# A softmax over 32768 columns: transfers of whole half rows in three buffers, in an order written out

## The chip, the core and the metric

The kernel runs on one core of one Trainium2 chip. The metric is the device time of one execution in microseconds (us). Three executions of the kernel before took 2491.85, 2492.3 and 2493.0 us; the median is 2492.3 us.

## The reference, cut to what matters

```python
logits = np.random.randn(16, 256, 32768).astype(np.float32); temperature = 1.0
scaled = logits / temperature
scaled = scaled - scaled.max(axis=-1, keepdims=True)
exp_scaled = np.exp(scaled)
return (exp_scaled / exp_scaled.sum(axis=-1, keepdims=True)).astype(np.float32)
```

There are 4096 rows of 32768 float32 values. Each row is read once and written once: 536.87 MB in, 536.87 MB out.

## The kernel before, in words

A row of 32768 values is cut into two half rows of 16384 values (64 KB), and each half row lies in one of the 128 partitions of the on-chip memory. So 64 rows make a **group** of 128 half rows, 8.4 MB, and there are 64 groups (`G`). The two halves of a row lie in neighbouring partitions.

A group is loaded, worked on in place and stored as two **chunks** (`C` = 2) of 8192 columns: 128 partitions of 32 KB each, 4.2 MB. The on-chip tensor `X` holds six chunks (`_BUFS`), which is three groups. Chunk i lies in buffer i modulo 6.

All transfers, loads (`load`, L113) and stores (`store`, L128), are issued by SyncE, in one queue and in program order. The page calls SyncE's queue SPq. A load first waits until the store that used its buffer last has landed, and a store waits until VectorE has scaled its chunk. At the start six loads are issued. After that, the main loop issues for each chunk i its store and then the load of chunk i + 4 (`_LEAD`). The first and the last group are loaded, and the last one stored, in pieces of 4096 columns (`_EDGE`).

For each group (`compute`):
- VectorE takes the negated maximum of a chunk (L156), and ScalarE then replaces the chunk by the exponentials of its values less that maximum, and adds them up (L170). Each chunk has a maximum and a sum of its own.
- When ScalarE is done with the last chunk, VectorE exchanges the small results between the two partitions of a row (L183, a shuffle) and finds the maximum of the row (L187); ScalarE computes a correction factor for each chunk (L194); VectorE adds the corrected sums (L200) and takes the reciprocal (L212).
- VectorE multiplies each chunk by its factor and by the reciprocal (L221). This is what a store waits for.

VectorE works through one group after the other and waits in place for ScalarE before the shuffle. In the last group the three steps on columns go in four pieces of 4096 columns instead of two of 8192.

A transfer of 128 partitions is spread over the core's 16 DMA engines. Each of them moves eight rows, a row of the transfer being one packet, and then adds one to the transfer's semaphore, a packet of a few bytes which is called a count here. A transfer has landed when all 16 counts have arrived. Each engine goes through its own list and does not wait for the others.

Of the kernel before, what the change touches and what calls it, by code (L numbers as in the profile page):

```python
# [6 lines left out]


_CW = 8192
_BUFS = 6  # L10
_LEAD = 4
_EDGE = 4096


class Stream:
# [7 lines left out]

    def wait(self, *tokens):
        need = {}
        for t in tokens:
            for sem, value in t if isinstance(t, list) else [t]:
                key = id(sem)
                if value > max(self.seen.get(key, 0), need.get(key, (None, 0))[1]):
                    need[key] = (sem, value)  # L30
        for key, (sem, value) in need.items():
            self.engine.wait_ge(sem, value)  # L32
            self.seen[key] = value
# [4 lines left out]
        return (self.sem, self.count)  # L38


class Landing:


    def __init__(self, nc, name):
        self.sem = nc.alloc_semaphore(name)
        self.count = 0

    def add(self, instruction):
        self.count += 16
        instruction.then_inc(self.sem, 16)  # L50

    def token(self):
        return (self.sem, self.count)


@with_exitstack
def kernel(
# [6 lines left out]
    nc = tc.nc  # L64
    inv_t = 1.0 / float(temperature)
    P = nc.NUM_PARTITIONS
    fp32 = mybir.dt.float32
    Exp = mybir.ActivationFunctionType.Exp
    A = mybir.AluOpType
# [1 line left out]
    xf = logits.flatten_outer_dims()  # L71
    of = out.flatten_outer_dims()
    N, V = xf.shape
    W = V // 2
    C = W // _CW
    assert W * 2 == V and C * _CW == W and (N * 2) % P == 0
    x = xf.rearrange("n (h v) -> (n h) v", h=2)
    o = of.rearrange("n (h v) -> (n h) v", h=2)
    G = N * 2 // P
    n_chunks = G * C  # L80
    swap = [i ^ 1 for i in range(32)]

    ctx.enter_context(tc.tile_critical())  # L83
    X = nc.alloc_sbuf_tensor("xs", [P, _BUFS * _CW], fp32)
    KM = 2 * C
    T = [nc.alloc_sbuf_tensor(f"t{q}", [P, 4 * KM], fp32) for q in range(2)]
    E = [nc.alloc_sbuf_tensor(f"ee{q}", [P, 2 * KM], fp32) for q in range(2)]
    J = [nc.alloc_sbuf_tensor(f"junk{q}", [P, 2 * KM], fp32) for q in range(2)]
    R = [nc.alloc_sbuf_tensor(f"row{q}", [P, 4], fp32) for q in range(2)]

    sp = Stream(nc, nc.sync, "sp")
    dve = Stream(nc, nc.vector, "dve")
    act = Stream(nc, nc.scalar, "act")
    loads = [[Landing(nc, f"ld{b}{h}") for h in range(_CW // _EDGE)] for b in range(_BUFS)]
    stores = [Landing(nc, f"st{b}") for b in range(_BUFS)]
    scaled = {}
    landed = {}
    fine = {}
    freed = {b: [] for b in range(_BUFS)}

    def spans(total, step):
        return [(s, min(step, total - s)) for s in range(0, total, step)]

    def load(i):
        g, c = divmod(i, C)
        b = i % _BUFS
        sp.wait(*freed[b])
        pieces = spans(_CW, _EDGE if g in (0, G - 1) else _CW)
        rows = slice(g * P, (g + 1) * P)
        for k, (s, n) in enumerate(pieces):  # L110
            lane = loads[b][k]
            lane.add(
                nc.sync.dma_start(  # L113
                    out=X[:, b * _CW + s : b * _CW + s + n],
                    in_=x[rows, c * _CW + s : c * _CW + s + n],
                )
            )
        landed[i] = [lane.token() for lane in loads[b] if lane.count]
        fine[i] = len(pieces) > 1

    def store(i):
        g, c = divmod(i, C)
        b = i % _BUFS
        rows = slice(g * P, (g + 1) * P)
        for s, n in spans(_CW, _EDGE if g == G - 1 else _CW):
            sp.wait(scaled[i, s])
            stores[b].add(
                nc.sync.dma_start(  # L128
                    out=o[rows, c * _CW + s : c * _CW + s + n],
                    in_=X[:, b * _CW + s : b * _CW + s + n],  # L130
                )
            )
        freed[b] = [stores[b].token()]

    hist = {}

    def compute(g):
        step = _EDGE if g == G - 1 else _CW
        per = _CW // step
        K = C * per  # L140
        t, e, j_, r = T[g % 2], E[g % 2], J[g % 2], R[g % 2]
        tv = t[:, 0 : 4 * K].rearrange("p (a b k) -> p a b k", a=2, b=2)
        old = hist.get(g - 2)
        sums = []
        for c in range(C):
            i = g * C + c
            b = i % _BUFS
            for s, n in spans(_CW, step):
                k = c * per + s // step
                xs = X[:, b * _CW + s : b * _CW + s + n]  # L150
                piece = s // _EDGE
                dve.wait(*(landed[i][piece : piece + 1] if fine[i] and step == _EDGE else landed[i]))
                if old:
                    dve.wait(old["ee"], old["tr"])
                m = dve.done(
                    nc.vector.tensor_reduce(  # L156
                        out=t[:, k : k + 1], in_=xs, axis=mybir.AxisListType.X, op=A.max, negate=True
                    )
                )
                if inv_t != 1.0:  # L160
                    dve.wait(m)
                    m = dve.done(
                        nc.vector.tensor_scalar_mul(
                            out=t[:, k : k + 1], in0=t[:, k : k + 1], scalar1=inv_t
                        )
                    )
                act.wait(m)
                sums.append(
                    act.done(
                        nc.scalar.activation(  # L170
                            out=xs,
                            in_=xs,
                            func=Exp,
                            bias=t[:, k : k + 1],
                            scale=inv_t,
                            accum_out=t[:, K + k : K + k + 1],
                        )
                    )
                )

        dve.wait(sums[-1])
        sh = dve.done(
            nc.vector.stream_shuffle(out=t[:, 2 * K : 4 * K], in_=t[:, 0 : 2 * K], mask=swap)  # L183
        )
        dve.wait(sh)
        mx = dve.done(
            nc.vector.tensor_reduce(  # L187
                out=r[:, 0:1], in_=tv[:, :, 0, :], axis=mybir.AxisListType.XY, op=A.min
            )
        )  # L190
        act.wait(mx)
        ev = e[:, 0 : 2 * K].rearrange("p (a k) -> p a k", a=2)
        ee = act.done(
            nc.scalar.activation(  # L194
                out=ev, in_=tv[:, :, 0, :], func=Exp, bias=r[:, 0:1], scale=-1.0
            )
        )
        dve.wait(ee)
        tr = dve.done(
            nc.vector.tensor_tensor_reduce(  # L200
                out=j_[:, 0 : 2 * K].rearrange("p (a k) -> p a k", a=2),
                in0=ev,
                in1=tv[:, :, 1, :],
                scale=1.0,
                scalar=0.0,
                op0=A.mult,
                op1=A.add,
                accum_out=r[:, 1:2],
            )
        )  # L210
        dve.wait(tr)
        rc = dve.done(nc.vector.reciprocal(out=r[:, 2:3], in_=r[:, 1:2]))  # L212
        dve.wait(rc)
        for c in range(C):
            i = g * C + c
            b = i % _BUFS
            for s, n in spans(_CW, step):
                k = c * per + s // step
                xs = X[:, b * _CW + s : b * _CW + s + n]
                scaled[i, s] = dve.done(  # L220
                    nc.vector.tensor_scalar(  # L221
                        out=xs,
                        in0=xs,
                        scalar1=e[:, k : k + 1],
                        scalar2=r[:, 2:3],
                        op0=A.mult,
                        op1=A.mult,
                    )
                )
        hist[g] = {"ee": ee, "tr": tr}  # L230

    for i in range(_BUFS):
        load(i)
    for g in range(G):
        compute(g)
        for c in range(C):
            i = g * C + c
            store(i)
            j = i + _LEAD
            if j >= _BUFS and j < n_chunks:  # L240
                load(j)
    sp.wait(*[s.token() for s in stores])


# [33 lines left out]
```

## Time and profile before

| What | us |
|---|---|
| three executions | 2491.85, 2492.3, 2493.0 |
| span of the profiled execution | 2493.0 |
| last instruction ends, from the span's start | 2492.96 |
| VectorE (DVE) busy | 1723.7 (69%) |
| ScalarE (ACT) busy | 944.5 (38%) |
| DMA queue 1, share of 16 engines | 99.9% |
| mean rate over the span | 431 GB/s |

| Instruction | tile | count | mean ns |
|---|---|---|---|
| maximum, L156 | 128x8192 | 126 | 8682 |
| maximum, L156 | 128x4096 | 4 | 4408 |
| exponential, L170 | 128x8192 | 126 | 7122 |
| exponential, L170 | 128x4096 | 4 | 3708 |
| scaling, L221 | 128x8192 | 126 | 4544 |
| scaling, L221 | 128x4096 | 4 | 2408 |

| Issue | count | KB each | us from issue to landing (median) |
|---|---|---|---|
| store | 126 | 4096 | 28.3 |
| load | 124 | 4096 | 38.9 |
| load | 8 | 2048 | 26.0 |
| store | 4 | 2048 | 15.5 |

The span runs from the first to the last instruction of one profiled execution; here it equals the highest of the three times. Busy time is the time that an engine spent in instructions; waiting is not counted. The DMA share is the time that packets took, as a share of 16 engines' time. The time from issue to landing includes the time that a transfer stood in the queue behind others. The trace also keeps a record of each packet: start, duration and size, but not which of the 16 engines moved it; where a text speaks of one engine's packets, they are those that follow on each other without a gap.

### The profile page before, as it was taken

Reading aid. Unit: us, or ns where it says so; the run is one execution under the profiler, and the core shown is the slowest. Engines: PE = TensorE matmul, PEld = TensorE weight load, DVE = VectorE, ACT = ScalarE, POOL = GpSimd, SP = SyncE. Lnnn points to the kernel's source line nnn. Section 1 sums busy time; section 2 is a strip of 40 time slices with the busy share of each in tenths; the row PEclk is TensorE's granted clock in tenths of the full one; section 3 lists DMA queues with packets and bytes.
Section 4 is the critical chain, followed back from the end, with each engine's and each line's share of the span. In section 5 each row is a group of like instructions: output and inputs, shape, how many; then the busy total and the mean of one; then the engine's idle time right before and its main releaser. Section 6 shows DMA issues by size and latency. Waiting matters only on the chain.

```text
span 2493.0 us, 1288 instructions
## 1 busy us (share of the span) xinstructions
DVE 1723.7 (69%) x644; ACT 944.5 (38%) x325; POOL 0.2 (0%) x4
## 2 busy tenths in 40 slices
DVE  6777667676676776767767667676676766767665
ACT  3443343433433334333343343433434334343342
POOL 0000000000000000000000000000000000000000
DMA  9999999999999999999999999999999999999998
GB/s 411 426 431 432 430 433 432 434 433 434 432 434 432 435 432 435 432 435 432 434 432 434 433 434 433 434 432 434 432 435 431 435 432 435 432 434 432 434 431 374
DMA packets 37738, 1073.84 MB, mean 431 GB/s; under 512 B 4192, under 2 KB 4192, under 8 KB 4192
## 3 DMA queue, kind: packets, MB, share of 16 engines
q1 hardware_dynamic: 37728, 1073.76, 99.9%
q14 instruction: 10, 0.08, 0.0%
HBM read 536.87 MB, written 536.87 MB: 431 GB/s over the span
## 4 chain that ended last, share of the span: by engine, by line
DMA 72%; DVE 20%; ACT 7%; issue 0%; SPq 0%; DVEq 0%
DMA xs<-in_logits_dram 40%; DMA out_dram<-xs 32%; DVE t L156 10%; DVE xs L221 9%; ACT xs L170 7%; ACT ee L194 0%; DVE row L212 0%; DVE row L187 0%; DVE t L183 0%; DVE junk L200 0%; SPq L113 0%; DVE row L200 0%; SPq L128 0%; SPq L273 0%; DVEq L32 0%
## 5 line engine op out<-in xcount | busy, mean ns | idle before, releaser
L170 ACT ACTIVATE xs<-xs,t 128x8192 f32<-128x8192 f32 (+1 forms) x130 | 912.1, 7016 | 1489.6 <-DVE t L156 1489.6
L156 DVE TENSOR_REDUCE t<-xs 128x1 f32<-128x8192 f32 (+1 forms) x130 | 1111.1, 8551 | 255.0 <-DMA xs<-in_logits_dram 255.0
L221 DVE TENSOR_SCALAR xs<-xs,ee,row 128x8192 f32<-128x8192 f32 (+1 forms) x130 | 576.6, 4478 | 2.3
L183 DVE LOAD_MASK_SELECT t<-t x64 | 0.9, 14 | 463.1 <-ACT xs L170 463.1
L194 ACT ACTIVATE ee<-t,row 128x4 f32<-128x4 f32 x64 | 19.0, 297 | 27.0 <-DVE row L187 27.0
L200 DVE CUSTOM_DVE_ANT_1 junk<-ee,t 128x4 f32<-128x4 f32 x64 | 10.4, 163 | 23.3 <-ACT ee L194 23.3
L170 ACT ACTIVATION_READ_ACCUMULATOR xs<-xs,t 128x1 f32 x130 | 24.2, 186 | 0.0
L212 DVE RECIPROCAL row<-row 128x1 f32<-128x1 f32 x64 | 10.5, 164 | 2.2
L187 DVE TENSOR_REDUCE row<-t 128x1 f32<-128x4 f32 x64 | 10.1, 157 | 2.2
L183 DVE STREAM_SHUFFLE t<-t 128x4 f32<-128x4 f32 x64 | 9.9, 155 | 0.0
L200 DVE DVE_READ_ACCUMULATOR2_ANT row<- 128x1 f32 x64 | 5.3, 82 | 0.0
L170 ACT ACT_TABLE_LOAD x1 | 1.3, 1283 | 0.9 <-SPq L83 0.9
L259 POOL MEMSET const-bfloat16-1.0<- 128x1 bf16 x1 | 0.1, 102 | 0.0
L259 POOL MEMSET const-uint8-127<- 128x1 uint8 x1 | 0.1, 101 | 0.0
L259 POOL MEMSET const-float32-0.0<- 128x1 f32 x1 | 0.1, 99 | 0.2 <-issue 0.2
L259 POOL MEMSET const-float32-1.0<- 128x1 f32 x1 | 0.1, 98 | 0.0
## 6 DMA issues: line engine op xcount, KB each, us to landing
out_dram<-xs SPq DMA_DIRECT2D x126, 4096.0 KB, 28.3
xs<-in_logits_dram SPq DMA_DIRECT2D x124, 4096.0 KB, 38.9
xs<-in_logits_dram SPq DMA_DIRECT2D x8, 2048.0 KB, 26.0
out_dram<-xs SPq DMA_DIRECT2D x4, 2048.0 KB, 15.5
```

The source lines that it names most:

```text
L156: nc.vector.tensor_reduce(out=t[:, k : k + 1], in_=xs, axis=mybir.AxisListType.X, op=A.max, negate=True)
L170: nc.scalar.activation(out=xs, in_=xs, func=Exp, bias=t[:, k : k + 1], scale=inv_t, accum_out=t[:, K + k : K + k + 1],)
L183: nc.vector.stream_shuffle(out=t[:, 2 * K : 4 * K], in_=t[:, 0 : 2 * K], mask=swap)
L187: nc.vector.tensor_reduce(out=r[:, 0:1], in_=tv[:, :, 0, :], axis=mybir.AxisListType.XY, op=A.min)
L194: nc.scalar.activation(out=ev, in_=tv[:, :, 0, :], func=Exp, bias=r[:, 0:1], scale=-1.0)
L200: nc.vector.tensor_tensor_reduce(out=j_[:, 0 : 2 * K].rearrange("p (a k) -> p a k", a=2), in0=ev, in1=tv[:, :, 1, :], scale=1.0, scalar=0. ...
L212: rc = dve.done(nc.vector.reciprocal(out=r[:, 2:3], in_=r[:, 1:2]))
L221: nc.vector.tensor_scalar(out=xs, in0=xs, scalar1=e[:, k : k + 1], scalar2=r[:, 2:3], op0=A.mult, op1=A.mult,)
L259: nc = _bacc.Bacc("TRN2", target_bir_lowering=False, num_devices=1)
```

## The change

- A transfer is a whole group, 128 half rows of 64 KB in one piece (`_W` = 16384 columns), where it was a chunk of 32 KB per partition. `X` has the same size, and holds three buffers of a group each.
- The order of all transfers is written out in `transfers`. After three loads come the store of group 0 in two halves and the load of group 3 in two halves; then the stores of groups 1 and 2. From group 4 on a load and the store of the group before it take turns. Near the end the loads of the last two groups stand back to back, and then come the last three stores, the last one in four pieces.
- The three steps on columns go in four pieces of 4096 columns (`_PIECE`) in every group. Each step is the same instruction as before, in the same order.
- A load waits for those stores of its buffer that overlap it, and a store for the scaled pieces that it covers. Semaphores are kept for each buffer and part.

```diff
-_CW = 8192
-_BUFS = 6
-_LEAD = 4
-_EDGE = 4096
+_W = 16384
+_BUFS = 3
+_PIECE = 4096
+_LAST_STORE = 4096
...
+def transfers(n):
+    half = _W // 2
+    whole = [(0, _W)]
+    halves = [(0, half), (half, half)]
+    quarters = [(s, _LAST_STORE) for s in range(0, _W, _LAST_STORE)]
+    plan = [("L", 0, whole), ("L", 1, whole), ("L", 2, whole)]
+    plan += [("S", 0, halves), ("L", 3, halves), ("S", 1, whole), ("S", 2, whole)]
+    for i in range(4, n - 2):
+        plan += [("L", i, whole), ("S", i - 1, whole)]
+    plan += [("L", n - 2, whole), ("L", n - 1, whole)]
+    plan += [("S", n - 3, whole), ("S", n - 2, whole), ("S", n - 1, quarters)]
+    return plan
...
-    X = nc.alloc_sbuf_tensor("xs", [P, _BUFS * _CW], fp32)
+    X = nc.alloc_sbuf_tensor("xs", [P, _BUFS * _W], fp32)
...
+    def overlapping(parts, s, n):
+        return [token for (a, m), token in parts.items() if a < s + n and s < a + m]
...
+        for k in range(K):
+            s = k * _PIECE
+            xs = X[:, base + s : base + s + _PIECE]
+            dve.wait(*overlapping(landed[g], s, _PIECE))
...
-    for i in range(_BUFS):
-        load(i)
-    for g in range(G):
-        compute(g)
-        for c in range(C):
-            i = g * C + c
-            store(i)
-            j = i + _LEAD
-            if j >= _BUFS and j < n_chunks:
-                load(j)
-    sp.wait(*[s.token() for s in stores])
+    for what, g, parts in transfers(G):
+        base = (g % _BUFS) * _W
+        rows = slice(g * P, (g + 1) * P)
+        if what == "L":
+            landed[g] = {}
+            for k, (s, n) in enumerate(parts):
+                if g >= _BUFS:
+                    sp.wait(*overlapping(stored[g - _BUFS], s, n))
+                landed[g][s, n] = loads.add(
+                    (g % _BUFS, k),
+                    nc.sync.dma_start(out=X[:, base + s : base + s + n], in_=x[rows, s : s + n]),
+                )
+            compute(g)
+        else:
+            stored[g] = {}
+            for k, (s, n) in enumerate(parts):
+                sp.wait(*overlapping(scaled[g], s, n))
+                stored[g][s, n] = stores.add(
+                    (g % _BUFS, k),
+                    nc.sync.dma_start(out=o[rows, s : s + n], in_=X[:, base + s : base + s + n]),
+                )
+    sp.wait(*stores.tokens())
```

More of the change, by code (lines that the diff above doesn't have):

```diff
@@ L25, in wait @@
         need = {}
[L26 to L30, printed above, removed]
+        for sem, value in tokens:
+            key = id(sem)
+            if value > max(self.seen.get(key, 0), need.get(key, (None, 0))[1]):
+                need[key] = (sem, value)
         for key, (sem, value) in need.items():
@@ L38, in done, with add, tokens @@
         return (self.sem, self.count)
-class Landing:
+class Lanes:
     def __init__(self, nc, name):
[L45 to L53, printed above, removed]
+        self.nc = nc
+        self.name = name
+        self.sems = {}
+        self.counts = {}
+    def add(self, key, instruction):
+        if key not in self.sems:
+            self.sems[key] = self.nc.alloc_semaphore(f"{self.name}_{'_'.join(map(str, key))}")
+            self.counts[key] = 0
+        self.counts[key] += 16
+        instruction.then_inc(self.sems[key], 16)
+        return (self.sems[key], self.counts[key])
+    def tokens(self):
+        return [(self.sems[k], self.counts[k]) for k in self.sems]
+def transfers(n):
[10 more added lines that the diff above has]
+    return plan
 @with_exitstack
@@ L73 @@
     N, V = xf.shape
-    W = V // 2
-    C = W // _CW
-    assert W * 2 == V and C * _CW == W and (N * 2) % P == 0
+    assert V == 2 * _W and (N * 2) % P == 0
     x = xf.rearrange("n (h v) -> (n h) v", h=2)
@@ L79 @@
     G = N * 2 // P
-    n_chunks = G * C
+    K = _W // _PIECE
     swap = [i ^ 1 for i in range(32)]
     ctx.enter_context(tc.tile_critical())
-    X = nc.alloc_sbuf_tensor("xs", [P, _BUFS * _CW], fp32)
[L85 to L88, printed above, removed]
+    X = nc.alloc_sbuf_tensor("xs", [P, _BUFS * _W], fp32)
+    T = [nc.alloc_sbuf_tensor(f"t{q}", [P, 4 * K], fp32) for q in range(2)]
+    E = [nc.alloc_sbuf_tensor(f"ee{q}", [P, 2 * K], fp32) for q in range(2)]
+    J = [nc.alloc_sbuf_tensor(f"junk{q}", [P, 2 * K], fp32) for q in range(2)]
     R = [nc.alloc_sbuf_tensor(f"row{q}", [P, 4], fp32) for q in range(2)]
@@ L93 @@
     act = Stream(nc, nc.scalar, "act")
-    loads = [[Landing(nc, f"ld{b}{h}") for h in range(_CW // _EDGE)] for b in range(_BUFS)]
-    stores = [Landing(nc, f"st{b}") for b in range(_BUFS)]
+    loads = Lanes(nc, "ld")
+    stores = Lanes(nc, "st")
+    landed = {}
+    stored = {}
     scaled = {}
[L97 to L133, printed above, removed]
     hist = {}
+    def overlapping(parts, s, n):
+        return [token for (a, m), token in parts.items() if a < s + n and s < a + m]
     def compute(g):
-        step = _EDGE if g == G - 1 else _CW
-        per = _CW // step
-        K = C * per
+        base = (g % _BUFS) * _W
         t, e, j_, r = T[g % 2], E[g % 2], J[g % 2], R[g % 2]
@@ L143, in compute @@
         old = hist.get(g - 2)
-        sums = []
-        for c in range(C):
-            i = g * C + c
[L147 to L154, printed above, removed]
+        if old:
+            dve.wait(*old)
@@ L155, in compute @@
+        sums = None
+        for k in range(K):
+            s = k * _PIECE
+            xs = X[:, base + s : base + s + _PIECE]
+            dve.wait(*overlapping(landed[g], s, _PIECE))
+            m = dve.done(
+                nc.vector.tensor_reduce(
+                    out=t[:, k : k + 1], in_=xs, axis=mybir.AxisListType.X, op=A.max, negate=True
+                )
+            )
+            if inv_t != 1.0:
+                dve.wait(m)
                 m = dve.done(
-                    nc.vector.tensor_reduce(
-                        out=t[:, k : k + 1], in_=xs, axis=mybir.AxisListType.X, op=A.max, negate=True
-                    )
-                )
@@ L160, in compute @@
[L160 to L178, printed above, removed]
-                )
@@ L181, in compute @@
-        dve.wait(sums[-1])
+                    nc.vector.tensor_scalar_mul(
+                        out=t[:, k : k + 1], in0=t[:, k : k + 1], scalar1=inv_t
+                    )
+                )
+            act.wait(m)
+            sums = act.done(
+                nc.scalar.activation(
+                    out=xs,
+                    in_=xs,
+                    func=Exp,
+                    bias=t[:, k : k + 1],
+                    scale=inv_t,
+                    accum_out=t[:, K + k : K + k + 1],
+                )
+            )
@@ L182, in compute @@
+        dve.wait(sums)
         sh = dve.done(
@@ L213, in compute @@
         dve.wait(rc)
[L214 to L228, printed above, removed]
-                )
@@ L230, in compute @@
-        hist[g] = {"ee": ee, "tr": tr}
-    for i in range(_BUFS):
-        load(i)
-    for g in range(G):
-        compute(g)
-        for c in range(C):
-            i = g * C + c
-            store(i)
-            j = i + _LEAD
-            if j >= _BUFS and j < n_chunks:
-                load(j)
-    sp.wait(*[s.token() for s in stores])
+        scaled[g] = {}
+        for k in range(K):
+            s = k * _PIECE
+            xs = X[:, base + s : base + s + _PIECE]
+            scaled[g][s, _PIECE] = dve.done(
+                nc.vector.tensor_scalar(
+                    out=xs,
+                    in0=xs,
+                    scalar1=e[:, k : k + 1],
+                    scalar2=r[:, 2:3],
+                    op0=A.mult,
+                    op1=A.mult,
+                )
+            )
@@ new lines, in compute @@
+        hist[g] = (ee, tr)
+    for what, g, parts in transfers(G):
+        base = (g % _BUFS) * _W
+        rows = slice(g * P, (g + 1) * P)
[7 more added lines that the diff above has]
+                    nc.sync.dma_start(out=X[:, base + s : base + s + n], in_=x[rows, s : s + n]),
+                )
+            compute(g)
[6 more added lines that the diff above has]
+                    nc.sync.dma_start(out=o[rows, s : s + n], in_=X[:, base + s : base + s + n]),
+                )
```

## The prediction

> **What bounds the kernel now.** I read the page's slices first. Each digit is the busy share of one fortieth of the span (62.3 us) in tenths.
>
> ```profile
> DVE  6777667676676776767767667676676766767665
> ACT  3443343433433334333343343433434334343342
> DMA  9999999999999999999999999999999999999998
> GB/s 411 426 431 432 430 433 432 434 433 434 432 434 432 435 432 435 432 435 432 434 432 434 433 434 433 434 432 434 432 435 431 435 432 435 432 434 432 434 431 374
> DMA packets 37738, 1073.84 MB, mean 431 GB/s; under 512 B 4192, under 2 KB 4192, under 8 KB 4192
> ```
>
> Seen here: VectorE idles a quarter of the time, the DMA engines never do; only the first three slices and the last move fewer bytes. The transfers bound the kernel, so the question is how long 16 engines need for a fixed 1073.7 MB. The 4192 small packets are semaphore counts, 16 for each of the 262 transfers.
>
> Second, what SyncE's queue waited for:
>
> ```profile
> SPq L128 <- DVE xs L221: 2207.9, 130, 39.9
> SPq L113 <- DMA out_dram<-xs: 153.7, 58, 3.3
> ```
>
> These waits cost nothing while transfers are queued ahead: the page's issue table has a store landing a median 28.3 us after issue, three transfers of 9.7 us.
>
> Third, the trace's packet records, in which one engine's packets follow on each other (start to start, ns): a 32 KB packet 1209.5, a 16 KB packet 607.1, a semaphore count 5.8. So a packet costs 2 x 607.1 - 1209.5 = 4.7 ns beside its bytes. An engine of this kernel handles 2000 packets of 32 KB, 96 of 16 KB and 262 counts: 2419.0 + 58.3 + 1.5 = 2478.8 us. Its first packet starts at 2.0; 2.0 + 2478.8 = 2480.8. But most engines end at 2485.4 and **the last at 2491.3**; 1.7 us later the span ends, 2493.0. So the end is set by one engine that lost 10.5 us on its way. Where:
>
> ```profile
> 58.00:62.00 4.00, 4.00 (x1) 4.00 (x1) 0.00 (x0) 1.00 0.96 303
> 99.00:103.00 4.00, 2.04 (x1) 2.62 (x3) 0.00 (x0) 1.00 1.00 369
> 600.00:604.00 4.00, 0.00 (x0) 4.00 (x1) 0.00 (x0) 1.00 1.08 467
> ```
>
> These are windows of 4 us; the last column is GB/s. At 58 us the first store follows six loads: all engines turn from reading to writing HBM at once, and their first two packets take 1.3 to 2.2 us instead of 1.21. At 99 us, another such turn, it is weaker; by 600 us it is gone. Until 450 us nearly every turn from load to store (one per 19.4 us) has some slow packets, and engines that lose there fall behind the others: the spread between the first and the last engine's count of one transfer grows from 0.9 us at 72 us to 5.3 us at 344 us, and then only slowly, to 8.4 us at the end (half of these last 3 us in two jumps beside instruction fetches).
>
> Fourth, the end:
>
> ```profile
> 2460.00:2465.00 5.00, 3.25 (x8) 1.54 (x3) 0.00 (x0) 1.00 0.84 360
> 2465.00:2470.00 5.00, 5.00 (x3) 0.00 (x0) 0.00 (x0) 1.00 0.91 387
> 2485.00:2490.00 5.00, 0.00 (x0) 0.00 (x0) 0.00 (x0) 1.00 0.17 72
> ```
>
> Near 2464 most engines idle about 2 us for the last group's first scaled piece; the late engine doesn't. From 2485.4 on it is nearly alone.
>
> **The change, part by part.** The sum starts from the profiled span, 2493.0, which is the highest of the three times; their median is 0.7 less.
>
> (1) *Longer packets, fewer counts.* By the same line a 64 KB packet takes 2 x 1209.5 - 4.7 = 2414.2 ns. An engine then has 125 transfers of 8 packets of 64 KB, plus S0 and L3 (S and L: store and load of a group) in halves, 16 each, and the last store in quarters, 32: 1064 packets instead of 2096, and 133 counts instead of 262. Saved: 1032 x 4.7 = 4.9 us, and 129 x 5.8 ns = 0.7 us: **-5.6**. All of it is on the path, since the late engine is never idle. No row shows 64 KB, so: at worst such a packet costs as two of 32 KB (saving 0.7 alone); at best nothing beside its bytes, 2409.6 (another 4.7). I take the straight line, the rows' own.
>
> The Trainium skill speaks against the edit here: "DMA: Bandwidth & Descriptors", section "Why small descriptors are slow (HBM only)", gives a fixed cost of about 3 cycles per packet and says that joining pieces pays only up to 256 B. The trace agrees with the cost, and at 4.7 ns in 1209 its verdict means 0.4%, which is small but all that there is to win here. By the verdict the sum would be 2493.0.
>
> (2) *SyncE's order in the steady state.* It issues L(i), S(i-1), L(i+1), S(i). A transfer is 8 x 2.414 + 0.006 = 19.32 us. When L(i) ends on an engine, S(i-1) and L(i+1) follow, 38.64 us, before S(i) is due. The cost of a group in four pieces stands at the end of this trace:
>
> ```profile
> 2440.01 17.39 DVE L156 TENSOR_REDUCE t<-xs 128x1 f32<-128x4096 f32 x4
> 2461.05 0.19 ACT L170 ACTIVATION_READ_ACCUMULATOR xs<-xs,t 128x1 f32 x1
> 2462.41 9.38 DVE L221 TENSOR_SCALAR xs<-xs,ee,row 128x4096 f32<-128x4096 f32 x4
> ```
>
> From 2440.01 to 2471.79 is 31.8 us. Add landing (last packet ends 2491.31, its count arrives 2491.76: 0.45) and issue (first load issued 0.95, first packet 1.97: 1.0): S(i) can start 33.3 us after L(i) ended. **Slack 5.4 us, cost 0.** Behind S(i) on SyncE stands L(i+2), due 19.3 us later still, and its buffer's store S(i-1) landed before. VectorE needs 31.8 of 38.6 us and is free when a load lands. Were the cover gone, each group would pay the excess, 64 times. The four pieces also add 126 x 0.19 us of ScalarE and some short starts, hidden by the same slack. For engines ahead of the last one the slack is 5.4 minus their lead; they wait then, at no cost, as the late one sets the end.
>
> (3) *Start.* L0 lands at 2.0 + 0.6 (slow first packets) + 19.3 + 0.45 = 22.3. VectorE then works through three groups, to 117.7; S2 can start at 118.7. Due: 2.6 + six transfers of 19.3 + 1.1 for the turn at 60 us = 119.6. Slack 0.9, cost 0. S0's first half is ready at 22.3 + 24.8 + 2.4 = 49.5, due at 60.5.
>
> (4) *End.* L62, L63, S61, S62, then S63. When L62 lands, VectorE works 31.8 us on group 62 and 24.8 us to group 63's first scaled piece (2440.01 to 2464.8). Ready after 0.45 + 31.8 + 24.8 + 1.0 = 58.05; the three transfers between last 57.96. **+0.1**; the later quarters take 4.9 us each against 2.4 for a scale. The 2 us at 2464 vanish, but the late engine did not have them.
>
> The 0.45 is not the empty end's alone: over all 4192 counts, in the full queue too, the arrival comes 0.28 to 0.78 us after the count's packet ends, at the median 0.35.
>
> The Trainium skill ("DMA: Bandwidth & Descriptors", section "Latency and other measured facts") puts HBM access latency at 2 us under high load, as the largest part of a completion. The trace, under full load, shows no count so late, and the measurement decides. By the page's figure (an estimate) every landing would be about 1.5 us later, S63 as much, and the sum 1.5 us more.
>
> (5) *What the late engine loses, 10.5 us.* Not shown for long packets. The early 5.3 us come from turns; I keep them. The late drift of 3 us has its size per packet or per time: 0 to -3 if it goes; I take half, **-1.5**.
>
> Sum: 2493.0 - 5.6 + 0.1 - 1.5 = 2486.0 for the span; 0.7 less for the median: **2485.3**.
>
> **Rivals.**
> A, *slower*: the turns stay costly. In the kernel before, spread reached 5.3 us before slow packets ended, and was free to reach 8.4, as two transfers more were queued. Now leads over 5.4 us are cut, because all engines ahead wait for the same S(i) and start it together. Price: 0.31 us per turn for the late engine (4.4 us over the 14 turns from 72 to 344 us); for 48 further turns +15: 2500. From 0.14 us per turn on the gain is gone. For it: that window at 58 us. Against: ten engines within 0.7 us of each other turn without a slow packet after 450 us.
> B, *not what it says*: rows are cut into 32 KB packets, or a long one costs as two: -0.7, drift kept: 2491.7. For: no row of 64 KB. Against: all 33,536 data packets here are whole rows of a transfer.
> C, *longer gain*: half as many turns in the early stage cost half, -2.7, and the drift goes, -1.5 more: 2481. Against: the loss ends when engines are spread, which may need as many turns.
>
> **How the numbers follow.** Forecast 0.52 (its own range 2482 to 2488.5), C 0.13, B 0.12, A 0.23 (a starved S(i) counted in). 0.2% is 5 us, about what a measurement of this kernel can tell from no change: under 2487.3 is faster. The forecast gives 0.45 to faster and 0.07 to same: faster 0.45 + 0.13 = 0.58, same 0.07 + 0.12 = 0.19, slower 0.23. Range 2480 to 2499: some 0.05 of C lies below, and the upper half of A, 0.12, above.
>
> **What would show it.** Data packets of 64 KB near 2418 ns long (a 32 KB one shows 1213), 17,024 of them and the smaller ones together, 2128 counts. SyncE's store waits end before the queue is empty: in the middle no slice under 433 GB/s. Slow packets at turns stop by some 500 us; if they go on, A. The last engine ends within 4 to 8 us of the median one. A dip near 119 us or before the last quarter stores would show (3) or (4) wrong; a dip in each group, (2).

## The result, and the profile after

The changed kernel takes 2512.63 us at the median (2510.53 to 2513.76, four executions), the kernel before 2492.65 (2491.85 to 2493.07, four): a ratio of 1.0078, 95% interval 1.0063 to 1.0092. It is **20 us slower**, where 7 us faster was forecast, and lies outside the range.

The changed kernel's page, rates in fortieths of its span of 2512.0 us, and the packets:

```profile
GB/s 409 443 427 432 434 432 432 425 432 432 420 433 425 429 431 422 432 424 430 433 421 431 434 427 425 434 431 422 433 432 421 431 422 433 433 420 432 434 420 389
DMA packets 19165, 1073.86 MB, mean 427 GB/s; under 512 B 2128, under 2 KB 2128, under 8 KB 2128
```

The packets came out as the change says: 17,024 of data and 2128 counts. But the rate, steady at 432 to 435 before, now dips to 420 again and again, from the eighth slice on. The answer for longer windows shows it more cleanly (first columns: window, its length; last column: GB/s). The kernel before:

```profile
550.00:1050.00 500.00, 347.48 (x130) 189.62 (x65) 0.00 (x0) 1.00 1.00 433
1050.00:1550.00 500.00, 346.10 (x131) 191.43 (x65) 0.00 (x0) 1.00 1.00 433
1550.00:2050.00 500.00, 345.53 (x130) 191.44 (x65) 0.00 (x0) 1.00 1.00 433
```

The changed kernel:

```profile
300.00:550.00 250.00, 174.67 (x94) 93.78 (x57) 0.00 (x0) 1.00 1.00 432
550.00:1050.00 500.00, 351.70 (x180) 201.56 (x117) 0.00 (x0) 1.00 1.00 428
1050.00:1550.00 500.00, 351.67 (x175) 197.75 (x115) 0.00 (x0) 1.00 1.00 428
1550.00:2050.00 500.00, 347.90 (x180) 193.64 (x113) 0.00 (x0) 1.00 1.00 428
```

Until 550 us the two are alike. Then the changed kernel loses 1.2% of its rate, for good, and yet the DMA share stays at 1.00: the engines do not idle, their packets take longer. The records of packets say where. I add up, per engine, what packets took beyond their usual time (611, 1213 and 2418 ns for 16, 32 and 64 KB), counting those over 40 ns late; this sum is called the **loss** below. Before, it is 3.8 us per engine, 3.1 of it in the first 250 us and none after 500. In the changed kernel it is 29.1 us, about 3 in every 250 us to the end. Most lies on the last packet before a turn: after 500 us, about 13 us on the last packet of a store with a load behind it, about 7 on the last packet of a load with a store behind it (an engine's packets taken as those that follow on each other, so the split is not exact).

What changed at 550 us is the **spread**, the time from the first to the last engine's count of one transfer. It grows to 6.1 us at 527 us, as it grew to 5.3 before, but then it stays mostly between 5 and 6 (4.9 to 6.6), and nine to twelve of the 16 engines end most transfers within 0.5 us of the first. Before, it grew on to 8.4, with seven engines within 0.5 us.

The end of the changed kernel:

```profile
2480.00:2485.00 5.00, 1.80 (x1) 4.47 (x3) 0.00 (x0) 1.00 0.97 419
2485.00:2490.00 5.00, 3.85 (x8) 0.94 (x3) 0.00 (x0) 1.00 0.21 92
2505.00:2510.00 5.00, 0.00 (x0) 0.00 (x0) 0.00 (x0) 1.00 0.89 377
2510.00:2515.00 5.00, 0.00 (x0) 0.00 (x0) 0.00 (x0) 1.00 0.00 0
```

Near 2486 the twelve leading engines wait 4 us for the last group's first quarter. The late ones don't, and so all end within 0.7 us of 2510. There is no late engine left to blame: every engine lost its 30 us or so on the way. Little of that is standing idle. By an estimate, the counts of the last transfer come at 2510.2; less the start at 2.0, 2473.2 us of undisturbed packets and 29.1 us of loss, some 6 us are left for an engine, 4 of them at 2486 for most.

SyncE's waits:

```profile
SPq L223 <- DVE xs L193: 2385.7, 68, 47.6
SPq L214 <- DMA out_dram<-xs: 55.5, 4, 25.7
```

SyncE sits ahead of the stores nearly all the time (2385.7 us), as before. What is different can't be read here: how long before its due time a store is issued.

### The profile page after: what moved, and what is told of

Same layout as the page of the kernel before. It is cut to its first block, busy times and chain, and to the rows that moved or that the text cites. A ratio compares the mean times of both kernels' runs of the same rounds, so it can differ in the third digit from the quotient of the medians.

```text
span 2512.0 us, 1661 instructions
## 1 busy us (share of the span) xinstructions
DVE 1755.7 (70%) x896; ACT 993.5 (40%) x577; POOL 0.2 (0%) x4
## 2 busy tenths in 40 slices
DMA packets 19165, 1073.86 MB, mean 427 GB/s; under 512 B 2128, under 2 KB 2128, under 8 KB 2128
## 4 chain that ended last, share of the span: by engine, by line
DMA 57%; DVE 36%; ACT 5%; SPq 0%; issue 0%
DMA xs<-in_logits_dram 56%; DVE t L133 23%; DVE xs L193 12%; ACT xs L146 5%; DMA out_dram<-xs 1%; ACT ee L168 0%; SPq L223 0%; DVE row L186 0%; DVE row L161 0%; DVE t L157 0%; DVE junk L174 0%; DVE row L174 0%; SPq L256 0%; SPq L100 0%
## 5 line engine op out<-in xcount | busy, mean ns | idle before, releaser
L146 ACT ACTIVATE xs<-xs,t 128x4096 f32<-128x4096 f32 x256 | 949.2, 3708 | 1464.4 <-DVE t L133 1464.4
L133 DVE TENSOR_REDUCE t<-xs 128x1 f32<-128x4096 f32 x256 | 1113.4, 4412 | 462.1 <-DMA xs<-in_logits_dram 462.1
L193 DVE TENSOR_SCALAR xs<-xs,ee,row 128x4096 f32<-128x4096 f32 x256 | 600.4, 2409 | 2.3
L146 ACT ACTIVATION_READ_ACCUMULATOR xs<-xs,t 128x1 f32 x256 | 47.7, 186 | 0.0
L168 ACT ACTIVATE ee<-t,row 128x8 f32<-128x8 f32 x64 | 19.2, 301 | 27.6 <-DVE row L161 27.6
L174 DVE CUSTOM_DVE_ANT_1 junk<-ee,t 128x8 f32<-128x8 f32 x64 | 10.7, 167 | 23.6 <-ACT ee L168 23.6
L186 DVE RECIPROCAL row<-row 128x1 f32<-128x1 f32 x64 | 10.5, 164 | 2.2
L161 DVE TENSOR_REDUCE row<-t 128x1 f32<-128x8 f32 x64 | 10.3, 161 | 2.2
L157 DVE STREAM_SHUFFLE t<-t 128x8 f32<-128x8 f32 x64 | 10.2, 160 | 0.0
```

Of the source, the lines that this page charges most:

```text
L133: nc.vector.tensor_reduce(out=t[:, k : k + 1], in_=xs, axis=mybir.AxisListType.X, op=A.max, negate=True)
L146: nc.scalar.activation(out=xs, in_=xs, func=Exp, bias=t[:, k : k + 1], scale=inv_t, accum_out=t[:, K + k : K + k + 1],)
L161: nc.vector.tensor_reduce(out=r[:, 0:1], in_=tv[:, :, 0, :], axis=mybir.AxisListType.XY, op=A.min)
L168: nc.scalar.activation(out=ev, in_=tv[:, :, 0, :], func=Exp, bias=r[:, 0:1], scale=-1.0)
L174: nc.vector.tensor_tensor_reduce(out=j_[:, 0 : 2 * K].rearrange("p (a k) -> p a k", a=2), in0=ev, in1=tv[:, :, 1, :], scale=1.0, scalar=0. ...
L193: nc.vector.tensor_scalar(out=xs, in0=xs, scalar1=e[:, k : k + 1], scalar2=r[:, 2:3], op0=A.mult, op1=A.mult,)
```

## The experiments

**Theory 1**: a store can be issued only 5.4 us before it is due (the *slack*). When the spread has grown to that, the leading engines run out of work, wait for the same store, and go on together; engines that turn together between loading and storing have slow packets. So the theory has two steps: engines are held, and being pushed together is what makes packets slow. **Theory 2**: a 64 KB packet makes a turn dear. **Theory 3**: the work in four pieces disturbs the transfers.

### Shorter packets, the same waits

```diff
 for what, g, parts in transfers(G):
+    together = len(parts) == 1
+    if together:
+        parts = [(0, _W // 2), (_W // 2, _W // 2)]
...
-    sp.wait(*overlapping(scaled[g], s, n))
+    sp.wait(*(scaled[g].values() if together else overlapping(scaled[g], s, n)))
```

The waits of loads on stores, and of compute on loads, are widened to both halves in the same way.

> The changed kernel with each whole transfer cut into two of 32 KB per partition, issued back to back and both behind the same waits; compute waits for both halves of a load. Order, slack and work stay, only the packet is shorter. Theory 1 (short slack: the store of a group can start only 5.4 us before it is due, so engines that lead by more are held and all turn from loading to storing together, and such bunched turns have slow packets): the loss stays, plus 1016 packets of 4.7 ns and 126 counts: about 2518 us (2512 to 2523), the spread of a transfer's counts stays under 6 us, slow packets at the turns to the end. Theory 2 (a 64 KB packet makes a turn dear, whatever the waits): as in the kernel before, 2490 to 2496 us, no slow packets after 500 us. Theory 3 (the work in four pieces disturbs the transfers): about 2518 us as well.

2518.44 us (2517.44 to 2521.64), ratio 1.0101 (1.0086 to 1.0116); spread about 5.4 us (4.6 to 6.2 after 600 us), loss 26.8 us. Theory 2 falls: packets of 32 KB lose as much under these waits.

### Stores in halves

```diff
-        plan += [("L", i, whole), ("S", i - 1, whole)]
+        plan += [("L", i, whole), ("S", i - 1, halves)]
```

and the same for the other whole stores.

> The changed kernel with all whole stores in two halves, each behind its own two scaled pieces; loads stay whole. The first half of a store can be issued 4.7 us earlier, so the slack is about 10 us instead of 5.4. Theory 1: no engine is held before the spread reaches 10 us, the slow packets end by about 600 us as before the change, and the time is 2 + 2473.1 + 2.7 (for 61 x 8 packets and 61 counts more per engine) + 10 for the late engine + 1.7 = 2489 us (2485 to 2494). Theory 2: loads keep their 64 KB packets, so half of the turn loss or more stays: 2500 to 2515. Theory 3: 2512 to 2517.

2511.47 us (2504.29 to 2512.52), ratio 1.0065 (1.005 to 1.008). The number forecast from theory 1 was missed by 22 us, and the time lies in the range given for theory 2, which the run before refutes. The windows of this kernel say why:

```profile
300.00:550.00 250.00, 174.67 (x94) 93.74 (x57) 0.00 (x0) 1.00 1.00 431
550.00:1050.00 500.00, 353.45 (x181) 201.57 (x117) 0.00 (x0) 1.00 1.00 432
1050.00:1550.00 500.00, 349.87 (x174) 199.76 (x115) 0.00 (x0) 1.00 1.00 429
1550.00:2050.00 500.00, 349.43 (x181) 193.02 (x114) 0.00 (x0) 1.00 1.00 428
```

The rate falls here too, but only after 1050 us. By then the spread has grown to 10.2 us, which is the larger slack, and there it stays; the loss per 250 us rises from 0.9 to between 2.4 and 3.2. More slack had only put it off. What I had wrong was that the spread would stop at 5.3 us.

### A shorter maximum

```diff
-    out=t[:, k : k + 1], in_=xs, axis=mybir.AxisListType.X, op=A.max, negate=True
+    out=t[:, k : k + 1], in_=xs[:, 0:512], axis=mybir.AxisListType.X, op=A.max, negate=True
```

> The changed kernel with each maximum taken over the first 512 of the piece's 4096 columns (it leaves out the rest of the maximum; the exponentials and sums stay). All transfers, packets and waits are those of the changed kernel, but the group takes about 27 us instead of 31.8, so the slack is about 10 us. Theory 1: the turn loss goes, 2 + 2473.1 + 9 + 1.7 = 2486 us (2482 to 2491), spread over 6 us. Theory 2: 2510 to 2514. Theory 3: the four pieces stay, 2508 to 2514.

2491.76 us (2490.32 to 2495.77), ratio 0.9994 (0.9985 to 1.0003). All transfers and packets are those of the changed kernel, and its 20 us are gone. Its windows:

```profile
550.00:1050.00 500.00, 162.56 (x182) 197.27 (x117) 0.00 (x0) 1.00 1.00 434
1050.00:1550.00 500.00, 162.54 (x182) 197.28 (x117) 0.00 (x0) 1.00 1.00 434
1550.00:2050.00 500.00, 161.31 (x182) 197.28 (x117) 0.00 (x0) 1.00 1.00 433
2050.00:2450.00 400.00, 128.64 (x145) 160.18 (x95) 0.00 (x0) 1.00 1.00 430
```

434 is the rate of long packets without the loss. The spread creeps to some 10 us by 1600 us and is 10.3 to 11.5 after 1900, close to the slack again, and the rate falls: the loss is 0.8, 1.7 and 2.3 us in the three stretches of 250 us from 1750 on. The profiled execution, 2495.77 us, is the slowest of ten, so most others may have lost less.

### Scaling later

```diff
+        late = dve.done(
+            nc.vector.tensor_reduce(
+                out=r[:, 3:4], in_=X[:, base : base + 2048], axis=mybir.AxisListType.X, op=A.max
+            )
+        )
+        dve.wait(late)
         scaled[g] = {}
```

> The changed kernel with one more maximum over 2048 columns (about 2.2 us, its result is not used) ahead of the scaling of each group: the slack falls from 5.4 to about 3.1 us, VectorE still needs less than a load and a store. Theory 1: the engines are held to a spread of some 3.5 us, bunch more, and lose more at each turn: 2516 to 2535 us. Theory 2 and theory 3: no change, 2511 to 2515.

2527.7 us (2521.25 to 2528.29), ratio 1.0137 (1.012 to 1.0154). The spread stays near 3.2 us (2.7 to 3.7 for most transfers), as theory 1 says, but the loss, 29.3 us, is that of the changed kernel: engines held tighter do not lose more at a turn. So the time lies in the range of theory 1, but not for its reason. The profiled execution took 2521.25 us, the least of the four; what came on top there, 7.5 us over that of the changed kernel, lies for the most part at the start, in this window of the kernel:

```profile
120.00:125.00 5.00, 5.00 (x4) 0.00 (x0) 0.00 (x0) 1.00 0.00 2
```

2 GB/s: the engines stand still for some 5.7 us, until VectorE has worked through three groups of 34 us and the third store can go. That is the point (3) of the prediction, with its cover gone. No trace shows where the other three executions lost 6 to 7 us more.

### Loads in halves

```diff
-        plan += [("L", i, whole), ("S", i - 1, whole)]
+        plan += [("L", i, halves), ("S", i - 1, whole)]
```

and the same for the last two loads.

> The changed kernel with the loads from group 4 on in two halves, so that the work on the first half runs beside the load of the second; stores stay whole, 64 KB. After a load has ended a group needs 23.4 us instead of 31.8: slack 13.8 us, for 2.7 us of packets and counts. Theory 1 as the first four runs left it (the spread between the engines grows until it fills the slack, and only then are the leading engines held, turn together and lose 0.4 to 0.5 us per turn to storing): the slack is filled after some 1500 us or not at all, so 2490 us without held engines, up to 2500 with a last third of held turns; the first half of the run shows no rise of the loss. Rival (transfers of 8.4 MB in turn lose at each turn, whatever the slack): 2505 to 2515, as with stores in halves.

2493.55 us (2492.61 to 2494.73), ratio 1.0004 (0.9994 to 1.0014). Two of its windows:

```profile
550.00:1050.00 500.00, 353.95 (x182) 197.82 (x116) 0.00 (x0) 1.00 1.00 434
1550.00:2050.00 500.00, 357.91 (x182) 201.55 (x117) 0.00 (x0) 1.00 1.00 434
```

The loss is 3.8 us, all but 0.3 of it before 500 us, and the spread, 9.5 us at the end, never fills the slack. The 20 us are gone, by two halves per load, with the full computation. The rival falls.

### The same with the shorter maximum

```diff
-        plan += [("L", i, whole), ("S", i - 1, whole)]
+        plan += [("L", i, halves), ("S", i - 1, whole)]
...
-    out=t[:, k : k + 1], in_=xs, axis=mybir.AxisListType.X, op=A.max, negate=True
+    out=t[:, k : k + 1], in_=xs[:, 0:512], axis=mybir.AxisListType.X, op=A.max, negate=True
```

> As the run with half loads, and each maximum over the first 512 columns of a piece alone (it leaves out the rest of the maximum): slack about 18 us, with stores of 64 KB. Theory 1: never filled, 2486 to 2492 us, no bunching of the engines before the last group. Rival: 2500 or more.

2493.02 us (2492.68 to 2493.68), ratio 0.9999 (0.999 to 1.0008): loss 3.0 us, spread 8.8 us, no sign of held engines, but 1 us over the expectation. Here slack beyond 14 us bought nothing that can be told from the scatter of the executions.

### Loads and stores in halves

```diff
-        plan += [("L", i, whole), ("S", i - 1, whole)]
+        plan += [("L", i, halves), ("S", i - 1, halves)]
```

and the same for the other whole stores and the last two loads.

> The changed kernel with loads from group 4 on and all whole stores in halves, each behind its own pieces: every packet is 32 KB or less, as in the kernel before, and the slack is about 18.5 us. Order and the work in four pieces are those of the changed kernel. Theory 1: the time of the kernel before, 2490 to 2497 us. Rivals (the order with two loads back to back, or the work in four pieces, loses the time): 2505 or more.

2497.0 us (2494.89 to 2499.44), ratio 1.0016 (1.0007 to 1.0025): loss 4.6 us. So neither the order with two loads back to back nor the four pieces cost the 20 us; theory 3 falls. The 4 us over the kernel before go with a late engine: the spread reached 13 us, in a profiled execution that was the slowest of ten (2499.44 us).

### The kernel before, with its stores held

```diff
-        pieces = spans(_CW, _EDGE if g in (0, G - 1) else _CW)
+        pieces = spans(_CW, _EDGE)
...
+        if i + 3 in landed:
+            sp.wait(landed[i + 3][0])
         for s, n in spans(_CW, _EDGE if g == G - 1 else _CW):
             sp.wait(scaled[i, s])
```

> The kernel before with all loads in two pieces of 4096 columns, and each store held until the first piece of the load ahead of it in the queue has landed: a store can then start only 3.5 us before it is due, where it had 15 us or more. The pieces cost 124 x 8 packets of 4.7 ns and 124 counts, 5.4 us: 2499 us if nothing else changes. Theory 1: the engines are held to a spread of 4 us and turn together at each of 128 turns to storing, 2515 to 2560 us. Rival (the loss belongs to the changed kernel's long transfers or pieces): 2496 to 2502 us.

2557.0 us (2552.79 to 2558.57), ratio 1.0256 (1.024 to 1.0271). Its windows:

```profile
550.00:1050.00 500.00, 337.99 (x122) 183.91 (x62) 0.00 (x0) 1.00 1.00 419
1050.00:1550.00 500.00, 337.51 (x130) 184.21 (x63) 0.00 (x0) 1.00 1.00 422
```

The loss is 60.9 us per engine, the spread 3.4 us. With the control that follows, the change's loss has been made in the kernel before, by a wait alone. There are twice as many turns as in the changed kernel, and the loss is twice as large.

### Its control

This one has the first line of the diff above (`pieces = spans(_CW, _EDGE)`) and no added wait.

> The kernel before with all loads in two pieces of 4096 columns and no store held: the control for the run with held stores. Theory 1: the pieces cost 5.4 us and nothing else changes, 2496 to 2502 us, spread growing freely past 5 us. Rival (short load pieces or more transfers in the queue bring the turn loss): 2515 to 2557.

2499.93 us (2499.58 to 2502.38), ratio 1.0029 (1.0018 to 1.0039): 7.0 us against the 5.4 worked out, loss 2.9 us, spread 10.1 us at the end.

```profile
550.00:1050.00 500.00, 345.71 (x130) 190.03 (x65) 0.00 (x0) 1.00 1.00 432
```

The short pieces and the added transfers are not it; the wait is.

### The kernel before, with its loads held

```diff
-        sp.wait(*freed[b])
+        sp.wait(*freed[b], *ahead[-1:])
...
-        for s, n in spans(_CW, _EDGE if g == G - 1 else _CW):
-            sp.wait(scaled[i, s])
+        for k, (s, n) in enumerate(spans(_CW, _EDGE)):
+            sp.wait(scaled[i, s if g == G - 1 else 0])
...
+        ahead.append(stores[b][0].token())
```

A store here has a semaphore for each of its two pieces.

> The kernel before with all stores in two pieces of 4096 columns, and each load held until the first piece of the store ahead of it has landed: now a load can start only 3.5 us before it is due, and no store is held. 5.4 us for the pieces. If any hold that bunches the engines brings the loss (theory 1 in its general form), 2515 to 2560 us, spread under 4 us, and the slow packets stay at the turns to storing although the loads are held. If only engines that wait for a store and start it together lose, 2496 to 2505 us.

2620.03 us (2615.27 to 2623.83), ratio 1.0509 (1.0493 to 1.0524); spread 2.8 us, loss 122 us.

```profile
550.00:1050.00 500.00, 335.69 (x123) 176.70 (x60) 0.00 (x0) 1.00 1.00 414
```

Holding loads is dearer still, so it is not the store's wait as such. The time is far above the range expected, and half of the expectation fell: the slow packets do not stay at the turns to storing. Over 110 of the 122 us lie within loads, more in their middle (about 55) than on the last packet before a store (about 44), which I can't explain. Theory 1, which looks for slow packets at turns, does not cover this run.

### One drain, halfway

```diff
             store(i)
+            if i == 64:
+                sp.wait(stores[i % _BUFS].token(), *landed[i + _LEAD - 1])
             j = i + _LEAD
```

> The kernel before with one extra wait: after the store of chunk 64, halfway, SyncE waits until everything issued has landed, and then goes on as before. All 16 engines start again together, once, and from then on no engine is held (slack 15.6 us). If engines that run together lose at the turns, whether held or not, the start repeats itself: spread under 1.5 us after the drain, some 3 us of slow packets per engine within the next 300 us and none after, spread back at 4 to 5 us; time 2493 + 1.4 for the empty queue + up to 5, 2494 to 2502 us. If only an engine that is held at a late issue has slow packets, none follow the drain beyond its first packets, and the time is 2488 to 2495 us, as the late engine's lag is taken back once.

2502.24 us (2500.99 to 2504.2), ratio 1.0037 (1.0023 to 1.0051). The time is 0.2 us above the first of the two ranges. Here nothing is held after the drain. The spread falls to 0.8 us and grows again to 3.6 us 300 us later and 6.3 at the end of the hundred before 2000 us; the loss is 2.6 us in the 250 us with the drain and 0.3 in the next.

```profile
1250.00:1300.00 50.00, 35.62 (x11) 20.50 (x8) 0.00 (x0) 1.00 0.87 377
```

In the 50 us of the drain the engines are idle for 13%, some 6.5 us each. The start repeats itself in size. That engines together are enough is not shown by it: 1.8 of the 2.6 us fall on the first transfer after the empty queue, where a first packet is slow also at the kernel's start, and the 0.8 us left are little.

### What the runs say together

| kernel | slack, us | spread where it stays, or at the end | loss, us per engine | time, us |
|---|---|---|---|---|
| before, loads held | 3.5 | 2.8 | 122 | 2620.0 |
| before, stores held | 3.5 | 3.4 | 60.9 | 2557.0 |
| changed, scaling later | 3.1 | 3.2 | 29.3 | 2527.7 |
| changed, 32 KB packets | 5.4 | 5.5 | 26.8 | 2518.4 |
| **changed** | 5.4 | 5.5 | 29.1 | 2512.6 |
| changed, stores in halves | 10.1 | 10.3 | 22.5 | 2511.5 |
| changed, shorter maximum | 10.2 | 10.3 to 11.5, from 1900 us | 9.3 | 2491.8 |
| changed, loads in halves | 13.8 | 9.5, not filled | 3.8 | 2493.6 |
| before | 15.6 | 8.4, not filled | 3.8 | 2492.7 |
| before, loads in pieces | 15.6 | 10.1, not filled | 2.9 | 2499.9 |
| changed, loads in halves, shorter maximum | 18 | 8.8, not filled | 3.0 | 2493.0 |
| changed, loads and stores in halves | 18.5 | 13, not filled | 4.6 | 2497.0 |

Spread and loss are those of the profiled execution, the time is the median of all. The slack is worked out as in the prediction, from durations; that of the kernel before is six transfers of 9.7 us less 42.5 us (19.4 until the group's other chunk is loaded, and 23.1 from there to the store). In the first seven kernels, five of the changed kind and two of the kernel before, the spread stops, at the median of its transfers, within 0.7 us of that number, and the loss runs where it has stopped. That holding is the cause is shown, by adding it and by taking it away.

How holding makes packets slow is not shown. That the engines are pushed together, the second step of theory 1, is an argument, and two counts speak against it as the whole reason. In the changed kernel the last four engines of a transfer, which reach its end 3 to 6 us after the first, lose as much as the rest: 22 to 25 us each from 600 to 2400 us, in the order in which engines end, where the other twelve lose 17 to 27. And the engines that end a transfer within 0.5 us of the first are 11 at the median in the changed kernel, but the number does not sort the kernels: 7 before and 8 with loads and stores in halves, without loss to speak of; 8 with the shorter maximum from 2000 us on, at 2.2 us of loss in 250 us; 7 with loads held, at 12 us in 250.

No record names the place in memory or the path. Nor do the runs tell whether an engine that has run dry adds something of its own at the turn that it waits for. At the other turn it can't: in the changed kernel the load is issued right behind the store, 19 us before it is due, and yet about 13 us of the loss lie there.

No version beats both kernels: loads in halves comes out even with the kernel before.

## Why the prediction was wrong, point by point

- **What bounds the kernel**, the transfers on 16 engines and a late one at the end: right for the kernel before.
- **(1) Longer packets, -5.6 us: right.** A 64 KB packet follows on the last after 2414.2 ns, the number worked out from 16 and 32 KB. The Trainium skill, in "DMA: Bandwidth & Descriptors", section "Why small descriptors are slow (HBM only)", gives a fixed overhead of about 3 cycles per packet. It gives them without a clock, so that the trace agrees, as the prediction has it, can be said of the kind alone: a fixed cost of a few ns, 4.7 here. With the loads in halves the gain can be seen: the median engine ends at 2483.4 instead of 2485.8 us, on which 2.9 us were to be expected for half of the packets. It does not reach the end, as the last engine is at 2491.2 (2491.8 before).
- **(2) The step that failed**: "Slack 5.4 us, cost 0", with "They wait then, at no cost, as the late one sets the end". The slack was right, as the spread stopped at it. The cost was not. The forecast asked only whether a held engine delays the last one, and put holding at nothing because the late engine waits for no one. What the runs showed in its place: while engines are held, packets turn slow on all of them, the late ones too, 29.1 us per engine where it was 3.8, and that is the 20 us. The window at 58 us, and the end of the slow packets once the engines had spread, were signs that the cost need not be nothing; only rival A used them. Why holding does it stays open.
- **(3) Start, 0: right**, no dip at 119 us: the window from 115 to 120 us moved 511 GB/s and the next 472. **(4) End, +0.1: right** for the late engine; the 4 us at 2486 are the leading engines'.
- **(5) The late engine's loss**, "I keep them" and -1.5 for the drift: this is the term through which (2) came in. Last packet at 2510.4, less the start at 2.0 and 2473.2 of undisturbed transfers, leaves 35.2 us instead of 10.5, **+24.7**. With it the sum is 2493.0 - 5.6 + 0.1 + 24.7 = 2512.2, and the span is 2512.0; since the term is taken from the end of the same execution, the sum must come out and is no check. The packets are one: their loss rose by 29.1 - 3.8 = 25.3 us per engine.
- **The median**: 0.7 us was taken off, as the span equals the highest of three times. That is chance: in the later runs an execution's time is 1.8 us above its span (2513.76 for 2512.0), so the profiled execution before took some 2494.8 us and was probably none of the three. After the change the median lies 0.6 us above the profiled span instead of 0.7 below. That is 1.3 us, not the cause.
- **Rival A** had the holding and its sign, at 0.23: against it I had counted ten engines that turn together without a slow packet. The count was right to within 0.05 us up to 1400 us (nine engines after that), and the runs do not explain it. Its price was too low, 0.31 us per turn to storing. The loss is 3 us per 250 us, 6.5 groups, so 0.46 us per group; A had 15 us in all, on top of a gain of 7. It too put the loss on engines that start a store together; more of it lies at the turn to loading.
- B (packets cut) is refuted by the page's packets. C's longer gain did not come.

## What to carry to other kernels

A transfer that is issued just before it is due is not free, even when no engine ever runs dry for long: count for each transfer how long before its due time it can be issued, and compare that with the spread of the DMA engines' counts, not with zero. Here 5 to 10 us were too little and 14 were enough, and splitting a load in two, so that work starts on the first half, bought the difference. The longer transfers saved 4.7 ns per packet here, and took 10 us of such slack.

## What the runs showed of the hardware that I had not expected

- The 16 engines drift apart by 5 us in the first 400 us and then by some 3 us more, and it pays to let them: free to drift they run at 432 to 434 GB/s, held by late stores at 428 with turns every 19 us and at 419 to 422 with turns every 10.
- A DMA share of 1.00 does not tell 434 from 428 GB/s, since a slow packet counts as busy. The rate over windows of 250 us or more does. In windows of 5 us long packets spoil it: the changed kernel shows 498 GB/s from 1015 to 1020 us, then 393 from 1035 to 1040.
- With no held engine the spread still reached 13 us in one kernel (loads and stores in halves) and 8.4 to 10.1 in others. What makes one engine so late is open.
- The Trainium skill says, in "DMA: Bandwidth & Descriptors", section "Anatomy of one DMA — SWDGE (gpsimd) path", that DMA engines do not wait on semaphores but consume their queues, while the wait sits on the issuing sequencer. The held stores agree: one wait of SyncE held all leading engines, and the spread stayed at 3.4 us where it grew to 10.1 in the control.
